# Scatter in one run and a runtime branch moved to the 13th expert block, in a two-layer mixer and MoE trunk

## The chip, the cores and the metric

The kernel runs on one core of a Trainium2 chip. The metric is device time in microseconds (us) of one execution. The kernel before takes 858.16 us, the median of three runs (857.32 to 858.34). One more execution was profiled; it took 858.35 us, and its trace covers a span of 856.6 us.

## The reference

The trunk has two layers for 256 tokens of width 1024, all in float32. A layer has a token mixer (one input projection; a causal convolution branch and a pooling branch, merged by gates; an output projection) and then a routed mixture of experts:

```
h2 = modulate(rms_norm(x, ffn_norm_g[l]), sh2, sc2)
x  = x + g2[:, None, :] * hierarchical_moe(h2, ...)

# hierarchical_moe: top-1 of 4 groups, top-2 of the 8 experts in it
combine = sum(one_hot(expert_id, 32) * weights[..., None], axis=1)
act = silu(t @ w_g[e]) * (t @ w_u[e])            # 1024 -> 256 per expert
out = out + (act * combine[:, e]) @ w_d[e]       # 256 -> 1024
```

So each token uses two of 32 experts. Each expert has 3 MB of weights, which every execution reads from HBM: about 101 MB per layer.

## The kernel before

**Layer.** `mixer` does the first half of a layer. `route` then finds each token's experts, gives every (token, expert) pair a place in a packed list of 512 columns sorted by expert, and gathers the normalised tokens into those columns (`XTp`, two tiles, tags `wl0` and `wl1`). `experts` and the function `blocks` that it returns do the rest.

**Blocks.** The 32 experts are worked in 16 blocks of two (`b` = 0 to 15). An expert has a window of 64 packed columns (`CAP`). `window(b)` (L1044, ScalarE) copies both windows into `XTW[b % 2]`. A block then does, on TensorE: gate/up (L1106, 32 matmuls, two 64-column halves of the array side by side), two transposes of the activated result (L1121), and down (L1081, 16 matmuls in two halves of 512 output columns). ScalarE and VectorE work between them: `sl` is silu (L1115) times up times routing weight (L1116), `aT` is the copy of the transposes (L1123), `gain` (L1087, L1088) multiplies down's result by the layer's gain and rounds it to a high part `yh`, `rest` (L1092) makes the low part `yl`.

**Scatter.** A block's 128 result rows go back to their tokens by a matrix of zeros and ones (`GT`, made by `prep`, L1052 and L1053). There are four parts, two halves of the columns for each of two token tiles; `scatter(b, part)` does two matmuls each (L1061 with `yh`, L1062 with `yl`), and `add(b, part)` (L1069, VectorE) adds the result to the residual `xs`. The scatter of block b - 1 is done in block b: parts 0 and 1 between gate/up and the transposes, parts 2 and 3 between the transposes and down. Parts and down share the PSUM pool `pd` of three buffers, except in the last block, whose parts 2 and 3 take `pa`.

**Overflow.** If an expert has over 64 tokens, its window doesn't hold them. `windows` (L821) computes a flag for that, and `overflow` (L977) loads it into a register of TensorE, ScalarE, VectorE and GpSimd (L980) and branches over a long body (L981) that would work all 32 experts for the tokens left out. On these inputs the body isn't run: the trace has none of its instructions. `overflow` is called at the end of `experts` (L1180), ahead of `blocks`. The body's weight loads go through GpSimd's queue; its working memory is `XTW[1]` and a tile of tag `xn`, the tag that `yhl` has in the blocks.

**Order.** In `route` and in the body of `experts` the order on TensorE, VectorE, ScalarE and GpSimd is the written one (`manual_schedule`). In blocks 0 to 14 only TensorE's is; VectorE and ScalarE are ordered by the compiler's scheduler. The end of block 15 is written for all four. An `If` is one unit of the schedule.

**Loads.** SP issues all weight loads in one fixed order, into a ring of 14 buffers of 1 MB, with up to five spare places for most of the experts. A load is issued when `done` frees a buffer, and waits for the release. A block uses six: gate and up of both experts in two halves of the input rows (512 KB loads, L114), and two for down (L116). After layer 0's experts the loads of the next layer follow at once.

Of the kernel before, what the change touches and what calls it, by code (L numbers as in the profile page):

```python
# [42 lines left out]
         1: ((0, 0), (0, 1), 0, 1, 4, 2, 5, 3, 6, 7, (1, 0), (1, 1))}  # L43
DIV_DVE = {0, 1, 2, 3}
FILL = (12, 24)
TAPS1, TAPS2 = 7, 6
ON_DVE = {2, 4, 6, 8, 30, 32, 34, 35, 36, 38}

# [2 lines left out]
def trunk(ctx, tc, x, c, mixer_norm_g, w_ada, b_ada, w_in, conv_w, conv_b, conv_ln_g, conv_ln_b,  # L51
# [643 lines left out]
    def route(l, moe, out_mm, out_add):  # L695
# [8 lines left out]
        def rt(name, shape, dt=F32):  # L704
            n = 1
            for d in shape[1:]:
                n *= d
            w = n // 2 if dt == BF else n
            v = rtile[:, rtop[0]:rtop[0] + w]
            rtop[0] += w  # L710
            if dt != F32:
                v = v.bitcast(dt)
            return v.rearrange(*{2: ("p a -> p a",), 3: ("p (a b) -> p a b",), 4: ("p (a b c) -> p a b c",)}[len(shape)],
                               **dict(zip("abc"[:len(shape) - 2], shape[1:-1])))
# [13 lines left out]
        ov = rt("ov", [P, TT, NE])  # L728
        px = rt("px", [P, TT, NE])
        po = rt("po", [P, TT, 2, NE])  # L730
        pk = rt("pk", [P, TT, 2])
        code = rt("code", [P, 2, TT, 2])
        so = rt("so", [P, NE])
        si = rt("si", [P, NE], I32)
# [76 lines left out]
            nc.vector.tensor_reduce(out=dst, in_=po, axis=AX.X, op=OP.add)  # L811

        def place():
            pick(pk, r["rp"][:, :TT, :])
            for ch in range(NCHUNK):
                if ch:
                    nc.vector.tensor_scalar(pk, pk, float(-SPC), None, op0=OP.add)
                for tt in range(TT):
                    onehot(G2[:, ch], tt, pk[:, tt, :])

        def windows():  # L821
            nc.vector.tensor_scalar(so, r["rp"][:, 2, :], float(LAST), None, op0=OP.min)
# [35 lines left out]
                        nc.vector.tensor_scalar(dst, p[:, kk, :], s["A2"][:, k:k + 1], s["B2"][:, k:k + 1],  # L858
                                                op0=OP.mult, op1=OP.add)

        r = dict(XTp=XTp, rss=rss, lg=lg, lm=lm, gm=gm, em=em, O=O, ov=ov, po=po, code=code, si=si, rt=rt, fill=fill)
        out_mm(2, 0)
        out_mm(3, 0)
        out_add(0)
# [112 lines left out]
    def overflow(l, r, moe):  # L977
        s = L[l]
        eng = [E.PE, E.Activation, E.DVE, E.Pool]
        flag = nc.values_load(r["fl"][0:1, 0:1], engines=eng, min_val=0, max_val=1)  # L980
        with tc.If(flag > 0):  # L981
            xo = work.tile([P, 2, D], F32, name="xo", tag="xn")
            xn = xo[:, 0].rearrange("p (k m) -> p k m", k=KC)
            hT = xo[:, 1].rearrange("p (k t) -> p k t", k=KC)
            wsp = r["XTW"][1].rearrange("p a c -> p (a c)")
            wov = r["lm"]
            nc.vector.tensor_tensor(wov, r["cw"][:, :, 0], r["cw"][:, :, 1], op=OP.add)
            nc.vector.tensor_tensor(wov, r["ov"], wov, op=OP.mult)
            for tt in range(TT):
                nc.scalar.activation(xn, xs[:, tt, :].rearrange("p (m k) -> p k m", k=KC), AF.Identity,  # L990
                                     scale=r["rss"][tt])
                for h in range(2):
                    p = pa([P, 4, P])
                    for kk in range(4):
                        nc.tensor.transpose(p[:, kk, :], xn[:, 4 * h + kk, :], ident)
                    for kk in range(4):
                        k = 4 * h + kk
                        nc.vector.tensor_scalar(hT[:, k, :], p[:, kk, :], s["A2"][:, k:k + 1], s["B2"][:, k:k + 1],
                                                op0=OP.mult, op1=OP.add)
                for e in range(NE):  # L1000
                    p = pa([P, 2, DE])
                    for i, wsrc in enumerate((w_expert_gate, w_expert_up)):
                        wv = wsrc[l, e].rearrange("(p k) h -> p k h", k=KC)
                        for h in range(2):
                            w = wsp.rearrange("p (k h) -> p k h", h=DE)
                            nc.gpsimd.dma_start(out=w, in_=wv[:, 4 * h:4 * h + 4, :])
                            for kk in range(4):
                                k = 4 * h + kk
                                nc.tensor.matmul(p[:, i, :], hT[:, k, :], w[:, kk, :], start=k == 0, stop=k == KC - 1)
                    sl = moe.tile([P, DE], F32, name="sl")  # L1010
                    nc.scalar.activation(sl, p[:, 0, :], AF.Silu)
                    ac = sl
                    nc.vector.scalar_tensor_tensor(ac, sl, wov[:, tt, e:e + 1], p[:, 1, :], op0=OP.mult, op1=OP.mult)
                    q = pt([P, 2, P])
                    for h in range(2):
                        nc.tensor.transpose(q[:, h, :], ac[:, h * P:(h + 1) * P], ident)
                    aT = moe.tile([P, 2, P], F32, name="aT")
                    nc.vector.tensor_copy(aT, q)
                    o = [pd([P, 512]) for _ in range(2)]
                    for h in range(2):  # L1020
                        nc.gpsimd.dma_start(out=wsp, in_=w_expert_down[l, e].rearrange("(j p) n -> p j n", p=P)[:, h])
                        for n in range(2):
                            nc.tensor.matmul(o[n], aT[:, h, :], wsp[:, n * 512:(n + 1) * 512], start=h == 0, stop=h == 1)
                    for n in range(2):
                        ns = slice(n * 512, (n + 1) * 512)
                        t = two.tile([P, 512], F32, name="ot", tag="part", bufs=3)
                        nc.vector.tensor_tensor(t, o[n], s["g2"][:, ns], op=OP.mult)
                        nc.vector.tensor_tensor(xs[:, tt, ns], xs[:, tt, ns], t, op=OP.add)


    def experts(l, r, moe):
# [23 lines left out]
        def scatter(b, part):  # L1055
            if b < 0:
                return
            h, tt = divmod(part, 2)
            hs = slice(h * 512, (h + 1) * 512)
            o = outs[part] = (pa if b == nb - 2 and part > 1 else pd)([P, 512])  # L1060
            nc.tensor.matmul(o, GTs[b][:, tt, :], ys[b][0][:, hs], start=True, stop=False)  # L1061
            nc.tensor.matmul(o, GTs[b][:, tt, :], ys[b][1][:, hs], start=False, stop=True)  # L1062

# [32 lines left out]
        def blocks():  # L1096
          with tc.manual_schedule(engines={E.PE}):
            for b in range(nb):
                p = pb([P, 2, DE])
                XT = XTW[b % 2]  # L1100
                for h in range(2):
                    w = need(*(("gu", l, 2 * b + j, h) for j in range(2)))
                    for kk in range(4):
                        k = 4 * h + kk
                        for j in range(2):
                            nc.tensor.matmul(p[64 * j:64 * j + 64], XT[:, k, 64 * j:64 * j + 64],  # L1106
                                             w[j][:, :, kk, :], start=k == 0, stop=k == KC - 1)
                    for j in range(2):
                        done(("gu", l, 2 * b + j, h))
                if b == 0:  # L1110
                    spread(r)
                    prep(0)
                window(b + 1)
                sl = moe.tile([P, DE], F32, name="sl", bufs=1)
                nc.scalar.activation(sl, p[:, 0, :], AF.Silu)  # L1115
                nc.vector.scalar_tensor_tensor(sl, sl, r["ws"][:, b:b + 1], p[:, 1, :], op0=OP.mult, op1=OP.mult)  # L1116
                scatter(b - 1, 0)
                scatter(b - 1, 1)
                q = pt([P, 2, P])
                for h in range(2):  # L1120
                    nc.tensor.transpose(q[:, h, :], sl[:, h * P:(h + 1) * P], ident)  # L1121
                aTs[b] = moe.tile([P, 2, P], F32, name="aT", bufs=1)
                nc.vector.tensor_copy(aTs[b], q)  # L1123
                add(b - 1, 0)
                add(b - 1, 1)
                scatter(b - 1, 2)
                scatter(b - 1, 3)
                add(b - 1, 2)
                add(b - 1, 3)
                prep(b + 1)  # L1130
                yhl = work.tile([P, 2, D], F32R, name="yhl", tag="xn")
                ys[b] = (yhl[:, 0, :], yhl[:, 1, :])
                if b == nb - 1:
                    break
                for n in range(2):
                    down(b, n)
                    gain(b, n)
                    rest(b, n)
                for j in range(2):
                    done(("ed", l, 2 * b + j))  # L1140
                if b == 5 and l + 1 < DEPTH:
                    small_mix(l + 1)
                if l + 1 == DEPTH and b in (5, 9):
                    final_gain(b)
# [32 lines left out]
        weights(l, r)  # L1177
        r["fill"](100)
        flush()
        overflow(l, r, moe)  # L1180
        return blocks


# [76 lines left out]
```

## Time and profile before

| | |
|---|---|
| time, median of 3 | 858.16 us |
| profiled execution | 858.35 us, span 856.6 us |
| TensorE busy | 775.5 us, 91% of the span |
| VectorE busy | 503.3 us, 59% |
| ScalarE busy | 279.7 us, 33% |
| GpSimd busy | 214.2 us, 25% |
| HBM read | 296.29 MB, 347 GB/s over the span |
| gate/up, L1106 | 912 matmuls, 228.1 us |
| down, L1081 | 512 matmuls, 160.6 us |
| adds, L1069 | 124, 82.1 us |
| GpSimd's load queue | 128 packets, 0.02 MB |

Matmuls are pipelined and overlap, so a matmul's own time (601 ns in gate/up) is longer than the step from one to the next. Layer 0's blocks run from about 210 to 436 us of the span, layer 1's from 618 to 845.

### The profile page before, as it was taken

The numbers are of one execution on the slowest core, as the hardware profiler recorded it, in microseconds if no ns is written. First come the engines' busy times: TensorE is split into PE (matmuls) and PEld (weight loads), VectorE is DVE, ScalarE is ACT, GpSimd is POOL, SyncE is SP. The second block draws the span as 40 slices with busy tenths as digits, with TensorE's granted clock in tenths as the row PEclk, the third lists the DMA queues.
The fourth block names the chain that finished last, engine by engine and source line by source line (L and its number), as shares of the span: only waits on it lengthen the run. The fifth ranks groups of instructions, "written<-read, shape, count | busy, mean of one in ns | idle before, by whom it ended". The sixth has DMA issues, their size and how long they took to land. (4 is left out here: it accounts for less than half of the span.)

```text
span 856.6 us, 12068 instructions
## 1 busy us (share of the span) xinstructions
PE 775.5 (91%) x4382; PEld 444.5 (52%) x4382; DVE 503.3 (59%) x1007; ACT 279.7 (33%) x496; POOL 214.2 (25%) x151
## 2 busy tenths in 40 slices
PE   4599999989799999999979999999679999999995
PEld 1389986755233333333339998686533333333332
DVE  2359984976245545454566998497734454535454
ACT  2254544454222122212135444545422212222212
POOL 1168972540000000000034799162100000000001
PEclk9699999999899999999988999999889999999998
DMA  9999958979999999999999965797679999999981
GB/s 350 371 355 390 390 172 335 353 250 404 404 406 409 408 409 366 354 409 410 404 380 382 397 226 186 283 385 248 241 249 372 383 410 409 409 409 409 409 347 49
DMA packets 100083, 298.28 MB, mean 348 GB/s; under 512 B 13941, under 2 KB 23461, under 8 KB 100010
## 3 DMA queue, kind: packets, MB, share of 16 engines
q1 hardware_dynamic: 99448, 296.30, 90.9%
q10 hardware_dynamic: 434, 1.06, 0.3%
q8 instruction: 38, 0.62, 0.3%
q14 instruction: 35, 0.29, 0.1%
q0 software_dynamic: 128, 0.02, 0.0%
HBM read 296.29 MB, written 1.05 MB: 347 GB/s over the span
## 5 line engine op out<-in xcount | busy, mean ns | idle before, releaser
L1106 PE MATMUL pb<-wt,XTW 128*64 128x512 f32 x912 | 228.1, 601 | 10.1 <-PEq L981 9.1
L427 POOL TENSOR_TENSOR wlo<-wt,whi 128x1024 fp32r<-128x1024 f32 x60 | 147.0, 2463 | 90.4 <-ACT whi L425 66.6
L1069 DVE TENSOR_TENSOR xs<-xs,pd 128x512 f32<-128x512 f32 x124 | 82.1, 684 | 134.8 <-PE pd L1062 133.6
L1106 PEld LDWEIGHTS pb<-wt,XTW 128*64 128x64 f32 x912 | 72.9, 139 | 132.2 <-issue 126.5
L486 DVE SCALAR_TENSOR_TENSOR pd<-vpad,cols,pd 128x256 f32<-128x256 f32 x232 | 106.9, 488 | 5.7
L425 ACT CAST whi<-wt 128x1024 fp32r<-128x1024 f32 x80 | 83.0, 1050 | 73.8 <-PE pb L365 40.8
L1088 ACT CAST yhl<-y 128x512 fp32r<-128x512 f32 x64 | 39.6, 620 | 195.1 <-DVE y L1087 195.1
L1081 PE MATMUL pd<-wt,aT 128*64 128x512 f32 x320 | 94.9, 598 | 0.9 <-DVE aT L1123 0.5
L1044 ACT COPY XTW<-XTp 128x256 f32 x128 | 48.3, 406 | 131.8 <-PE pb L1106 120.3
L1092 DVE TENSOR_TENSOR yhl<-y,yhl 128x512 fp32r<-128x512 f32 x64 | 44.3, 693 | 46.1 <-ACT yhl L1088 46.0
L364 PE MATMUL pa<-hhl,whi 128*128 128x256 f32 x224 | 66.5, 297 | 5.2 <-ACT hhl L399 5.2
L316 PE MATMUL pd<-wt,cb 128*32 128x512 f32 x384 | 54.3, 655 | 14.6 <-DMA wt<-in_w_ada_dram 14.5
L1081 PE MATMUL pd<-wx,aT 128*64 128x512 f32 x192 | 65.7, 598 | 0.5 <-DVE aT L1123 0.5
L365 PE MATMUL pa<-hhl,whi 128*128 128x256 f32 x224 | 65.8, 294 | 0.3
L366 PE MATMUL pa<-hhl,wlo 128*128 128x256 f32 x224 | 64.7, 289 | 0.7 <-POOL wlo L427 0.7
L364 PE MATMUL pb<-hhl,whi 128*128 128x256 f32 x224 | 63.6, 284 | 0.0
L365 PE MATMUL pb<-hhl,whi 128*128 128x256 f32 x224 | 62.7, 280 | 0.0
L366 PE MATMUL pb<-hhl,wlo 128*128 128x256 f32 x224 | 62.6, 279 | 0.0
L1061 PE MATMUL pd<-yhl,GT 128*128 128x512 f32 x124 | 54.9, 443 | 0.6 <-ACT yhl L1088 0.6
L1081 PEld LDWEIGHTS pd<-wt,aT 128*64 128x64 f32 x320 | 27.0, 136 | 52.8 <-issue 37.2
L1168 POOL TENSOR_TENSOR xn<-xs,fz 128x512 f32<-128x512 f32 x2 | 2.6, 1284 | 189.9 <-ACT xn L353 189.9
L1087 DVE TENSOR_TENSOR y<-pd,gb 128x512 f32<-128x512 f32 x64 | 44.0, 688 | 9.9 <-PE pd L1081 9.7
(260 smaller groups left out, 1249.7 us busy)
## 6 DMA issues: line engine op xcount, KB each, us to landing
wt<-in_w_expert_gate_dram SPq DMA_DIRECT2D x114, 512.0 KB, 7.1
wt<-in_w_expert_up_dram SPq DMA_DIRECT2D x114, 512.0 KB, 11.7
wt<-in_w_ada_dram SPq DMA_DIRECT2D x48, 1024.0 KB, 11.7
wt<-in_w_expert_down_dram SPq DMA_DIRECT2D x36, 1024.0 KB, 12.4
wt<-in_w_in_dram SPq DMA_DIRECT2D x28, 1024.0 KB, 13.9
wx<-in_w_expert_down_dram SPq DMA_DIRECT2D x24, 1024.0 KB, 12.7
wt<-in_w_out_dram SPq DMA_DIRECT2D x8, 1024.0 KB, 4.9
wx<-in_w_expert_gate_dram SPq DMA_DIRECT2D x14, 512.0 KB
```

Of the source, the lines that this page charges most:

```text
L316: nc.tensor.matmul(ps[j:j + 32, :], cb[:, 2 * i + a, :], halves(w[:, a, :], h), start=i == 0, stop=i == 3)
L364: nc.tensor.matmul(o, ah, bh, start=start, stop=False, skip_group_check=True)
L365: nc.tensor.matmul(o, ah, bl, start=False, stop=False, skip_group_check=True)
L366: nc.tensor.matmul(o, al, bh, start=False, stop=stop, skip_group_check=True)
L425: nc.scalar.copy(hi, wv)
L427: eng.tensor_tensor(lo, wv, hi.bitcast(F32), op=OP.subtract)
L486: nc.vector.scalar_tensor_tensor(acc[:, j, :] if t == CONV_K - 1 else a, src, w, a, op0=OP.mult, op1=OP.add)
L1044: nc.scalar.copy(XTW[b % 2][:, 4 * h:4 * h + 4, CAP * j:CAP * j + CAP], r["XTp"][h][:, :, bass.ds(v, CAP)])
L1061: nc.tensor.matmul(o, GTs[b][:, tt, :], ys[b][0][:, hs], start=True, stop=False)
L1069: nc.vector.tensor_tensor(xs[:, tt, hs], xs[:, tt, hs], outs.pop(part), op=OP.add)
L1081: nc.tensor.matmul(o[64 * j:64 * j + 64, :], aTs[b][:, h, 64 * j:64 * j + 64], wv[j][:, h, :], start=h == 0, stop=h == 1)
L1106: nc.tensor.matmul(p[64 * j:64 * j + 64], XT[:, k, 64 * j:64 * j + 64], w[j][:, :, kk, :], start=k == 0, stop=k == KC - 1)
```

## The change

Three edits. First, all four scatter parts of block b - 1 come between gate/up and the transposes of block b, and the four adds behind `aT`; parts 0 and 1 use the PSUM pool `pa` (two buffers), parts 2 and 3 `pd`. Second, `overflow` is called in `blocks`, ahead of block 12 (`LATE`), and the scatter of block 11 is done in front of it, so that block 12 has none. Third, the body of the branch works on the four sets of 128 packed columns in `XTp` instead of normalising the tokens anew; for that, `place` keeps both chunks' places in `pk`. The flag that decides on the body is computed as before.

```
+LATE = 12
...
-        pk = rt("pk", [P, TT, 2])
+        pk = rt("pk", [P, NCHUNK, TT, 2])
...
-            pick(pk, r["rp"][:, :TT, :])
+            pick(pk[:, 0], r["rp"][:, :TT, :])
             for ch in range(NCHUNK):
                 if ch:
-                    nc.vector.tensor_scalar(pk, pk, float(-SPC), None, op0=OP.add)
+                    nc.vector.tensor_scalar(pk[:, 1], pk[:, 0], float(-SPC), None, op0=OP.add)
                 for tt in range(TT):
-                    onehot(G2[:, ch], tt, pk[:, tt, :])
+                    onehot(G2[:, ch], tt, pk[:, ch, tt, :])
...
-            o = outs[part] = (pa if b == nb - 2 and part > 1 else pd)([P, 512])
+            o = outs[part] = (pa if part < 2 else pd)([P, 512])
...
             for b in range(nb):
+                if b == LATE:
+                    for part in range(4):
+                        scatter(b - 1, part)
+                        add(b - 1, part)
+                    overflow(l, r, moe)
                 p = pb([P, 2, DE])
...
-                scatter(b - 1, 0)
-                scatter(b - 1, 1)
+                if b != LATE:
+                    for part in range(4):
+                        scatter(b - 1, part)
                 q = pt([P, 2, P])
                 for h in range(2):
                     nc.tensor.transpose(q[:, h, :], sl[:, h * P:(h + 1) * P], ident)
                 aTs[b] = moe.tile([P, 2, P], F32, name="aT", bufs=1)
                 nc.vector.tensor_copy(aTs[b], q)
-                add(b - 1, 0)
-                add(b - 1, 1)
-                scatter(b - 1, 2)
-                scatter(b - 1, 3)
-                add(b - 1, 2)
-                add(b - 1, 3)
+                if b != LATE:
+                    for part in range(4):
+                        add(b - 1, part)
                 prep(b + 1)
...
         r["fill"](100)
         flush()
-        overflow(l, r, moe)
         return blocks
```

## Rows read from the trace of the kernel before

**Rows 1.** Chain of waits from 625 us on: shares by line, and one later piece.
```profile
by line: PE pb L1106 12.9%; PE pd L1081 6.5%; PE pd L1061 1.4%; DVE xs L1069 1.3%; PE pd L1062 1.1%; PE pt L1121 0.7%; DVE sl L1116 0.7%; PE pd L1195 0.2%; ACT xn L353 0.2%; DVE yhl L1092 0.2%; issue 0.2%; DVE y L1087 0.2%; PE pd L966 0.1%;
...
652.85 6.87 PE pb L1106 x32
```

**Rows 2.** Timeline, layer 1's block 1: start, us, instruction, count, [idle before, releaser].
```profile
645.99 0.50 PE L1061 MATMUL pd<-yhl,GT 128*128 128x512 f32 x1
...
646.56 0.40 PE L1061 MATMUL pd<-yhl,GT 128*128 128x512 f32 x1
...
646.76 0.69 DVE L1069 TENSOR_TENSOR xs<-xs,pd 128x512 f32<-128x512 f32 x1 [4.45 <-PE pd L1062]
646.80 0.39 PE L1062 MATMUL pd<-yhl,GT 128*128 128x512 f32 x1
...
647.36 0.47 DVE L1116 SCALAR_TENSOR_TENSOR sl<-sl,rtile,pb 128x256 f32<-128x256 f32 x1
647.75 0.68 DVE L1069 TENSOR_TENSOR xs<-xs,pd 128x512 f32<-128x512 f32 x1
...
647.89 0.44 PE L1121 MATMUL pt<-idc,sl 128*128 128x128 f32 x2 [0.71 <-DVE sl L1116]
...
648.37 0.42 DVE L1123 COPY aT<-pt 128x256 f32<-128x256 f32 x1
...
649.19 3.65 PE L1081 MATMUL pd<-wx,aT 128*64 128x512 f32 x16
```

**Rows 3.** Timeline, the last two blocks of layer 1.
```profile
825.55 0.50 PE L1061 MATMUL pd<-yhl,GT 128*128 128x512 f32 x1
...
828.17 3.65 PE L1081 MATMUL pd<-wt,aT 128*64 128x512 f32 x16 [0.17 <-DVE xs L1069]
...
838.62 0.50 PE L1061 MATMUL pd<-yhl,GT 128*128 128x512 f32 x1
...
838.74 0.39 ACT L1115 ACTIVATE sl<-pb 128x256 f32<-128x256 f32 x1 [5.20 <-PE pb L1106]
...
840.17 0.42 DVE L1123 COPY aT<-pt 128x256 f32<-128x256 f32 x1
...
841.00 3.65 PE L1081 MATMUL pd<-wt,aT 128*64 128x512 f32 x16
```

**Rows 4.** Timeline, TensorE around the branch of layer 1.
```profile
617.98 2.79 PE L1106 MATMUL pb<-wt,XTW 128*64 128x512 f32 x10 [1.02 <-ACT XTW L1044]
...
625.06 7.60 PE L1106 MATMUL pb<-wt,XTW 128*64 128x512 f32 x22 [4.30 <-PEq L981]
```

**Rows 5.** Line 981 by sequencer (q): count, ns minimum/median/maximum, first and last start.
```profile
L981 POOLq EVENT_SEMAPHORE  x8: 17/43/43, 203.4 to 612.1; - x8
L981 POOLq COMPARE_BRANCH  x2: 45/48/50, 197.9 to 609.3; - x2
...
L981 PEldq COMPARE_BRANCH  x2: 6102/6118/6133, 212.6 to 618.8; - x2
```

**Rows 6.** Line 980 on TensorE's sequencer.
```profile
L980 PEldq TENSOR_LOAD <-rtile x2: 310/400/490, 211.7 to 613.4; - x2
```

**Rows 7.** Stretches: busy us (count) by engine, then PEclk, DMA share, GB/s.
```profile
626.00:628.00 2.00, 2.00 (x8) 0.74 (x6) 0.60 (x4) 0.83 (x3) 0.00 (x0) 0.50 0.00 0
```

**Rows 8.** Page, part 2: GB/s in 40 slices of 21.4 us.
```profile
GB/s 350 371 355 390 390 172 335 353 250 404 404 406 409 408 409 366 354 409 410 404 380 382 397 226 186 283 385 248 241 249 372 383 410 409 409 409 409 409 347 49
```

**Rows 9.** Timeline, TensorE in layer 0: block 11's gate/up, and the end of block 15.
```profile
369.40 7.04 PE L1106 MATMUL pb<-wt,XTW 128*64 128x512 f32 x32
...
432.82 3.65 PE L1081 MATMUL pd<-wt,aT 128*64 128x512 f32 x16
...
438.97 0.51 PE L1062 MATMUL pd<-yhl,GT 128*128 128x512 f32 x1 [0.23 <-DVE yhl L1092]
```

**Rows 10.** Timeline of SP, layer 0: one load's issue.
```profile
354.56 0.33 SPq L114 DMA_DIRECT2D wt<-in_w_expert_up_dram  x1
```

**Rows 11.** Loads issued from 417 to 422 us: count, size each, median us to landing.
```profile
wt<-in_w_expert_down_dram SPq DMA_DIRECT2D x4, 512.0 KB, 10.4
```

More of the change, by code (lines that the diff above doesn't have):

```diff
@@ L859, in gather @@
                                                 op0=OP.mult, op1=OP.add)
-        r = dict(XTp=XTp, rss=rss, lg=lg, lm=lm, gm=gm, em=em, O=O, ov=ov, po=po, code=code, si=si, rt=rt, fill=fill)
+        r = dict(XTp=XTp, rss=rss, lg=lg, lm=lm, gm=gm, em=em, O=O, ov=ov, pk=pk, po=po, code=code, si=si, rt=rt, fill=fill)
         out_mm(2, 0)
@@ L982, in overflow @@
             xo = work.tile([P, 2, D], F32, name="xo", tag="xn")
[L983 to L999, printed above, removed]
+            wsp, y = xo[:, 0], xo[:, 1]
@@ new lines, in overflow @@
+            nc.vector.tensor_tensor(r["cw"], r["cw"], r["ov"][:, :, None, :].to_broadcast([P, TT, 2, NE]), op=OP.mult)
+            for c in range(2 * SEQ // P):
+                at = slice(c % 2 * P, c % 2 * P + P)
+                g = two.tile([P, TT, 2, P], F32, name="gp", tag="part", bufs=3)
+                for tt in range(TT):
+                    for i in range(2):
+                        nc.vector.tensor_scalar(g[:, tt, i, :], io256[:, at], r["pk"][:, c // 2, tt, i:i + 1], None,
+                                                op0=OP.is_equal)
+                pw = pt([P, NE])
+                for n in range(4):
+                    nc.tensor.matmul(pw, g[:, n // 2, n % 2, :], r["cw"][:, n // 2, n % 2, :], start=n == 0, stop=n == 3)
+                wv = two.tile([P, NE], F32, name="wv", tag="b2s", bufs=1)
+                nc.vector.tensor_copy(wv, pw)
+                gt = two.tile([P, TT, P], F32, name="gt", tag="part", bufs=3)
+                for tt in range(TT):
+                    nc.vector.tensor_tensor(g[:, tt, 0, :], g[:, tt, 0, :], g[:, tt, 1, :], op=OP.add)
+                    q = pt([P, P])
+                    nc.tensor.transpose(q, g[:, tt, 0, :], ident)
+                    nc.vector.tensor_copy(gt[:, tt, :], q)
+                o = [pd([P, 512]) for _ in range(2)]
@@ L1002, in overflow @@
                     for i, wsrc in enumerate((w_expert_gate, w_expert_up)):
-                        wv = wsrc[l, e].rearrange("(p k) h -> p k h", k=KC)
+                        wx = wsrc[l, e].rearrange("(p k) h -> p k h", k=KC)
                         for h in range(2):
                             w = wsp.rearrange("p (k h) -> p k h", h=DE)
-                            nc.gpsimd.dma_start(out=w, in_=wv[:, 4 * h:4 * h + 4, :])
+                            nc.gpsimd.dma_start(out=w, in_=wx[:, 4 * h:4 * h + 4, :])
                             for kk in range(4):
-                                k = 4 * h + kk
-                                nc.tensor.matmul(p[:, i, :], hT[:, k, :], w[:, kk, :], start=k == 0, stop=k == KC - 1)
+                                nc.tensor.matmul(p[:, i, :], r["XTp"][h][:, kk, c * P:(c + 1) * P], w[:, kk, :],
+                                                 start=h + kk == 0, stop=h + kk == 4)
                     sl = moe.tile([P, DE], F32, name="sl")
@@ L1012, in overflow @@
                     ac = sl
-                    nc.vector.scalar_tensor_tensor(ac, sl, wov[:, tt, e:e + 1], p[:, 1, :], op0=OP.mult, op1=OP.mult)
+                    nc.vector.scalar_tensor_tensor(ac, sl, wv[:, e:e + 1], p[:, 1, :], op0=OP.mult, op1=OP.mult)
                     q = pt([P, 2, P])
@@ L1018, in overflow @@
                     nc.vector.tensor_copy(aT, q)
-                    o = [pd([P, 512]) for _ in range(2)]
                     for h in range(2):
@@ L1022, in overflow @@
                         for n in range(2):
[L1023 to L1028, printed above, removed]
+                            nc.tensor.matmul(o[n], aT[:, h, :], wsp[:, n * 512:(n + 1) * 512],
+                                             start=e + h == 0, stop=e + h == NE)
+                for n in range(2):
+                    ns = slice(n * 512, (n + 1) * 512)
+                    nc.vector.tensor_tensor(y[:, ns], o[n], s["g2"][:, ns], op=OP.mult)
+                    for tt in range(TT):
+                        q = pa([P, 512])
+                        nc.tensor.matmul(q, gt[:, tt, :], y[:, ns], start=True, stop=True)
+                        nc.vector.tensor_tensor(xs[:, tt, ns], xs[:, tt, ns], q, op=OP.add)
     def experts(l, r, moe):
```

## The prediction, made before the result was known

> **What bounds the kernel now.** I read the chain of waits first: from the first expert block of the second layer to the end it runs along TensorE, through gate/up (L1106), down (L1081), scatter and transposes, with two VectorE instructions per block and no load in it [rows 1]. Then the timeline of one block [rows 2]. Gate/up ends at 645.99, the next down begins at 649.19. In these 3.20 us TensorE issues two scatter parts (four matmuls from 645.99 to 646.80, 0.24 apart once they run), waits 0.71 us for `sl`, transposes, issues two more parts and goes on. The wait is VectorE's: an add of 0.60 stands ahead of `sl` in its queue. Thirteen of a layer's sixteen blocks look like this; in the last two `sl` comes ahead of the add, and the gaps are 2.62 and 2.38 us [rows 3]. Third, the branch: after ten gate/up matmuls of block 0 TensorE of layer 1 stands 4.30 us behind its sequencer, whose branch takes 6.1 us in both layers [rows 4, 5]. It restarts at half clock: 22 matmuls take 7.60 us, against 22 x 0.215 = 4.73 at full clock (6.87 / 32 each) [rows 1, 4, 7]. Last the loads: layer 0's blocks, from 205 to 430 us, run on a saturated queue, 404 to 410 GB/s outside two slices, while in layer 1 the queue falls to 241 and 249 around the branch [rows 8].
>
> **The change part by part.** The sum is made against the profiled execution, 858.35 us (span 856.6 and 1.75 around it); the median shown is 0.19 below.
>
> *No branch at the start.* Without it the eleventh matmul would issue 0.22 after the tenth, which issues near 620.18 (its modelled end 620.77 less 0.59), not at 625.06: 4.7 us earlier. The clock loss, 7.60 - 4.73 = 2.9, goes too. I take 7.5 us, and the same for layer 0, where the branch is as long. What is late next is block 0's chain behind gate/up, which stays as it is. The eight mask instructions of `spread` on VectorE then run under gate/up.
>
> *Four scatter parts in one run.* From 645.99: four matmuls to 646.80, four more at 0.24 to 647.76, transposes at 648.00, `aT` 0.48 later as now (647.89 to 648.37), 0.42 of copy and 0.05, down at 648.95. The gap becomes 2.96: 0.24 saved in an ordinary block. `sl`, done at 647.75, hides under the scatter, but the cover that `aT` had, the two scatter parts behind the transposes, is gone: its 0.47 lies bare, and that is why so little is won. In the last two blocks 2.96 replaces 2.62 and 2.38, 0.34 and 0.58 lost. The parts that move to the other PSUM pool find it free, as nothing else in blocks 1 to 15 uses it. The second down half now takes the buffer of part 2 and waits for its add, which ends about 1.2 us after `aT` begins, under the 1.79 us of the first half. Blocks 1 to 11 give 11 x 0.24 = 2.6; blocks 13 to 15 together cost 0.34 + 0.58 - 0.24 = 0.7.
>
> *Block 12.* Let t be the end of down(11). The scatter of block 11 now runs with no gate/up over it. The last block of layer 0 shows that price: down begins at 432.82 and takes 3.6 (649.19 to the next gate/up), which ends it at 436.4, and the last scatter wait is met at 438.97, t + 2.57 [rows 2, 9]. Then the flag load and the branch: 0.9 from load to branch (211.7 to 212.6) and 6.1 [rows 5, 6], 0.2 to the first matmul: t + 9.8. The scatter's last matmuls end under it, so TensorE stands some 6 us and the clock falls: gate/up takes 6.87 + 2.8, to t + 19.5. No scatter follows, so the gap is the bare chain, 0.05 + 1.43 from `silu` to `aT` [rows 3] + 0.47: down(12) at t + 21.4. Before it began at t + 6.87 + 3.20 = t + 10.1, so the cost is 11.3. That is the upper end if TensorE keeps to the written order. But in the kernel before, ten gate/up matmuls that are written behind the branch ran ahead of it [rows 4]; five ahead would fill the time in which VectorE ends its adds, 1.1 us, for 10.2. Nothing tells between the two; I take 10.8. Below that lies only a cheaper branch, which is a rival. The other engines reach their branch at t + 2 (ScalarE) to t + 5 (VectorE) and need it past at t + 19. On POOL nothing of the blocks is queued behind it. SP has no branch; its loads behind block 12's releases come later, and the loads of more than two blocks are ahead of them (14 buffers, 6 per block).
>
> *The load queue.* In layer 1 it was not full at the start, because loads waited for block 0's buffers; an earlier start moves loads and matmuls together, and nothing is lost. In layer 0 it is saturated, so an earlier TensorE runs into it. Counted back from the layer's last, block 11's last gate/up load is issued at 354.56; at 10.4 us to landing it is there at 365.0, and TensorE wants it half way through gate/up, 369.40 + 3.43 = 372.8 [rows 9 to 11]. That is 7.9 us of lead, while the advance by then is 7.5 + 10 x 0.24 = 9.9. The two slices at 366 and 354 GB/s [rows 8] may partly fill up when buffers come free earlier, worth 0 to 2.5 us; I take 1. So 1.0 us of the advance is lost in layer 0.
>
> *The rest.* The copy of the places for the second chunk costs one small VectorE instruction, as before. The rewritten body runs nothing as long as the flag is zero, as now.
>
> Sum, layer 1: -7.5 - 2.6 + 0.7 + 10.8 = +1.4. Layer 0: the same and 1.0, +2.4; the next layer starts on the residual, so it passes on. Together +3.8, or 862.1 against 858.35, and **862.0** against the median. With the ends 10.2 and 11.3 for block 12 and 0 to 2.5 for the slices this case spans 860 to 864, and with 0.1 us of error in the gap (26 blocks) 857.5 to 866.5.
>
> [...]
>
> **Rivals.**
> *VectorE puts an add ahead of `aT`.* Its order in the blocks isn't written by hand. The second add ends at 648.37 [rows 2], `aT` would be ready at 648.48, and the third add, whose scatter is now early, is ready before both. If whoever is ready goes first, `aT` waits 0.5 more, and the gap is 3.46, 0.26 longer than now. For: the add that stands ahead of `sl` today. Against: the margin is 0.1 us, and in the last two blocks `aT` did come ahead of the second add. Price 14 x 0.5 = 7.0 per layer, less layer 0's 1.0, since nothing runs into the queue then: +3.8 + 14.0 - 1.0 = +16.8, 875.
>
> *The branch is cheaper at block 12: faster.* The skip isn't one price for all: POOL was past it in 2.8 us in layer 1 (609.3 to 612.1) and in 5.5 in layer 0 (197.9 to 203.4) [rows 5]. If TensorE's 6.1 were 2.8 there, 3.3 us go per layer, and up to 2.8 more if so short a stand leaves the clock up: 862 - 6.6 = 855.4 to 849.8, middle 853. It decides from 1.9 us per layer, a branch of 4.2. Against: TensorE took 6.1 with a saturated queue in layer 0 and with a queue running dry in layer 1, and block 12 has a saturated one.
>
> *The branch moves and costs the same.* Should the scheduler run gate/up(12) and the bare chain under the branch, block 12 costs about 8.5 to 9.5, and the kernel ends within 0.2% of before: 858.5.
>
> **How the numbers follow.** Forecast case 0.53, the add ahead of `aT` 0.25, the cheaper branch 0.13, the hidden one 0.09. A measurement of this kernel tells 0.2% (1.7 us) from no change. The forecast case, by its span, is slower in 0.36, the same in 0.13, faster in 0.04. The second case is slower; the third is faster but for 0.02; the fourth gives 0.06 same, 0.01 slower, 0.02 faster. Slower 0.62, same 0.21, faster 0.17. The range reaches from the upper end of the cheaper branch, 855, to just above the late `aT`, 876; the forecast's own is 857.5 to 866.5.
>
> **What would show it.** Right: no stand in block 0 and its gate/up at full clock; a gap of 2.96 with no wait for `sl`; in block 12 a stand of 5 to 6 us behind the sequencer and a clock of 0.5 after it; in layer 0 a short wait for gate/up weights near block 11. Wrong: an add between `sl` and `aT` twice over (second case); a branch far from 6.1 us; more than ten gate/up matmuls ahead of it; or a layer 0 that ends earlier than at 436 us, as its queue allows almost nothing.

## The result, and the profile after

The changed kernel takes 867.6 us (median of four runs, 865.2 to 869.8) against 858.16, the median of the three ordinary runs of before (a fourth took 1570.39 us and is left out): ratio 1.0108, 95% interval 1.009 to 1.0125. It is 9.4 us slower; 3.8 were forecast. A second measurement, beside the experiments, gave 1.0095 (1.0064 to 1.0127). The profiled execution is 867.54 us, 9.19 above that of before.

One row per step of the prediction, each from first matmul to first matmul (us, after minus before, from the two timelines; down(11) is the first down matmul of block 11):

```
                                    layer 0                   layer 1                  forecast
gather -> first down          22.77 - 29.98 =  -7.2    23.48 - 29.84 =  -6.4      -7.5
first down -> down(11)       147.31 - 150.19 = -2.9   148.67 - 152.25 = -3.6      -2.6 (+1.0 in layer 0)
down(11) -> down(12)          31.48 - 13.65 = +17.8    24.44 - 13.65 = +10.8     +10.8
down(12) -> down(15)          39.95 - 39.60 =  +0.4    39.96 - 39.55 =  +0.4      +0.7
sum                                           +8.1                     +1.2      +2.4, +1.4
```

One cell stands out, down(11) to down(12) in layer 0. Its ends, in the kernel before and in the changed one:

```profile
365.92 3.65 PE L1081 MATMUL pd<-wt,aT 128*64 128x512 f32 x16
379.57 0.64 PE L1081 MATMUL pd<-wt,aT 128*64 128x512 f32 x1
```
```profile
370.77 0.64 PE L1088 MATMUL pd<-wt,aT 128*64 128x512 f32 x1 [0.52 <-DVE aT L1136]
...
402.25 0.65 PE L1088 MATMUL pd<-wx,aT 128*64 128x512 f32 x2 [0.52 <-DVE aT L1136]
```

An ordinary block first, as in [rows 2] (timeline of layer 1's block 1 in the changed kernel: start, us, instruction, count, idle before and releaser):

```profile
647.27 0.50 PE L1068 MATMUL pa<-yhl,GT 128*128 128x512 f32 x1
...
648.65 0.47 DVE L1128 SCALAR_TENSOR_TENSOR sl<-sl,rtile,pb 128x256 f32<-128x256 f32 x1
...
649.02 0.39 PE L1069 MATMUL pd<-yhl,GT 128*128 128x512 f32 x1
649.04 0.68 DVE L1076 TENSOR_TENSOR xs<-xs,pa 128x512 f32<-128x512 f32 x1
...
649.24 0.38 PE L1134 MATMUL pt<-idc,sl 128*128 128x128 f32 x2
649.67 0.42 DVE L1136 COPY aT<-pt 128x256 f32<-128x256 f32 x1
650.01 1.27 DVE L1076 TENSOR_TENSOR xs<-xs,pd 128x512 f32<-128x512 f32 x2
...
650.14 1.08 PE L1088 MATMUL pd<-wx,aT 128*64 128x512 f32 x4 [0.52 <-DVE aT L1136]
```

Eight scatter matmuls in one run, no wait for `sl`, the third and fourth add behind `aT`, and 2.87 us from scatter to down where it was 3.20. Now the branch, by sequencer, as in [rows 5], and what TensorE does behind it in layer 0:

```profile
L982 PEldq COMPARE_BRANCH  x2: 5972/6036/6100, 378.3 to 792.8; - x2
```
```profile
384.74 1.09 PE L1118 MATMUL pb<-wx,XTW 128*64 128x512 f32 x1 [6.35 <-DMA wx<-in_w_expert_down_dram]
390.44 1.01 PE L1118 MATMUL pb<-wx,XTW 128*64 128x512 f32 x1 [4.62 <-issue]
390.57 1.09 PE L1118 MATMUL pb<-wt,XTW 128*64 128x512 f32 x1
```

TensorE stands 6.35 us at the branch (a load is named as releaser; at the same place in layer 1 it is the sequencer), issues one matmul and stands again for 4.62, waiting for nothing that the profile ties to it. In layer 1 the same code runs on:

```profile
799.13 1.08 PE L1118 MATMUL pb<-wx,XTW 128*64 128x512 f32 x1 [6.03 <-PEq L982]
799.26 1.09 PE L1118 MATMUL pb<-wt,XTW 128*64 128x512 f32 x1
800.01 1.06 PE L1118 MATMUL pb<-wx,XTW 128*64 128x512 f32 x1
```

The view of the DMA queues lists what moved in a stretch: packets, MB, share of 16 engines. Inside the second stand (384.7 to 390.4 us) there are rows of kind instruction, that is, of code, and the page's third part has q8 for the whole span:

```profile
q8 instruction: 1, 0.02, 1.4%
q14 instruction: 2, 0.02, 0.9%
```
```profile
q8 instruction: 39, 0.64, 0.3%
```

39 packets for 0.64 MB are pieces of 16 KB of code. In ordinary blocks a q8 packet comes every two blocks or so: from 226.2 to 362.3 us they are 26.5 to 28.3 us apart, with 234 to 254 matmuls and weight loads of TensorE from one to the next. Behind the branch of layer 0 they begin at 381.9 and 387.7, each 2.7 to 2.8 us ahead of a restart. That q8 brings TensorE's code is read from these times and counts; which engines q14 serves, with its smaller packets, isn't shown. And each restart finds the clock at half (busy us and count, then the granted clock, DMA share, GB/s):

```profile
384.70:385.90 1.20, 1.09 (x1) 0.50 1.01 403
390.40:394.00 3.60, 3.56 (x9) 0.50 1.02 408
394.00:402.20 8.20, 6.74 (x27) 0.88 1.03 409
```

### The profile page after: what moved, and what is told of

It reads as the page before. It is cut to its first block, busy times and chain, and to the rows that moved or that the text cites. A ratio compares the mean times of both kernels' runs of the same rounds, so it can differ in the third digit from the quotient of the medians.

```text
span 865.7 us, 12039 instructions
## 1 busy us (share of the span) xinstructions
PE 776.0 (90%) x4382; PEld 455.3 (53%) x4382; DVE 499.5 (58%) x1007; ACT 279.1 (32%) x496; POOL 214.2 (25%) x151
## 5 line engine op out<-in xcount | busy, mean ns | idle before, releaser
L1118 PEld LDWEIGHTS pb<-wt,XTW 128*64 128x64 f32 x912 | 76.2, 138 | 124.0 <-issue 119.0
L1076 DVE TENSOR_TENSOR xs<-xs,pa 128x512 f32<-128x512 f32 x64 | 43.3, 684 | 124.7 <-PE pa L1069 124.7
L1118 PE MATMUL pb<-wx,XTW 128*64 128x512 f32 x112 | 52.5, 638 | 17.0 <-DMA wx<-in_w_expert_down_dram 6.4
```

## The experiments

Theory A: the second stand is a second fetch of code. The branch lands four or five instructions before the end of a piece, and the next one is asked for only then. B: the second matmul waits for weights on the full queue. C: it belongs to the place, block 12 of layer 0. D: the branch's 6 us are the compare itself, not a fetch. The test for A is code that never runs. How far the landing point is from the end of its piece is an estimate: I counted it in the program, with the end put where the changed kernel stands. Where nothing else is said, a fence shows TensorE's timeline of the kernel named, in the columns above.

**Moving the landing point** (`shift16`, `shift248`, `move_stand`, `start_stand`). One edit, with other counts per layer:

```diff
         with tc.If(flag > 0):
+            pad = (4, 0)[l]    # shift248 (62, 0); move_stand (4, 23); start_stand (43, 0), branch at the start
+            if pad:
+                q = pt([P, P])
+                for n in range(pad):
+                    nc.tensor.matmul(q, ident, ident, start=n == 0, stop=n == pad - 1)
```

> The changed kernel with four more matrix products in the body of layer 0's branch, which the flag never lets run: 17 instructions of TensorE that shift where the code behind both branches lies and change nothing that runs. Theory A (the second stand of layer 0, 4.62 us behind the first matmul of block 12, is a second fetch of code: the branch lands four or five instructions before the end of a fetched 16 KB piece): the landing point is now past that end, the stand goes, block 12 of layer 0 costs about what it costs in layer 1, and the kernel takes 867.6 less 5.7 to 7.1: 861 us (860 to 862.5). Theory B (the second matmul waits for a load of weights on the full queue): the stand stays, 867 to 868. Theory C (the place at block 12 of layer 0, whatever the code): the same 867 to 868.

Measured: 863.2 us, ratio 1.0042 (1.0024 to 1.006), where the changed kernel has 1.0108 and 1.0095; that is 0.7 us above the upper end of the expectation, and the profiled execution, 861.1, is the fastest of its ten. No second stand; down(11) to down(12) takes 25.06 in layer 0.

```profile
382.85 1.08 PE L1123 MATMUL pb<-wx,XTW 128*64 128x512 f32 x1 [6.36 <-PEq L982]
382.97 1.09 PE L1123 MATMUL pb<-wt,XTW 128*64 128x512 f32 x1
383.73 1.06 PE L1123 MATMUL pb<-wx,XTW 128*64 128x512 f32 x1
```

The next piece still comes (one q8 packet between 382.8 and 390 us), but beside running matmuls. B and C fall: nothing that runs was changed.

> The changed kernel with 249 never-run instructions in layer 0's body, so that the landing point of layer 0 has some seven more instructions left in its 16 KB piece than in the changed kernel: eleven or twelve. Theory A, with sizes: the next piece comes as late as before, some 5.7 us behind the restart, so the second stand begins later by what the seven instructions run and is shorter by the same: 2.5 to 3.5 us instead of 4.62, and the step from down(11) to down(12) 28 to 30.5 us instead of 31.48 (25.0 without a second stand). If the landing point were only lucky and nothing were counted by pieces: 25 or 31.5.

Measured, in a single execution: 867.8 us; the second stand is 3.61, just above the forecast, the step 29.36.

```profile
385.81 1.06 PE L1123 MATMUL pb<-wt,XTW 128*64 128x512 f32 x1
390.48 1.01 PE L1123 MATMUL pb<-wx,XTW 128*64 128x512 f32 x1 [3.61 <-issue]
```

More matmuls run first, and the second restart comes 5.73 us after the first (384.75), as in the changed kernel (5.70): the next piece takes the same time (in the changed kernel its q8 packet begins 5.8 us behind the first one's), the stand is what is left of it.

> The changed kernel with never-run matrix products in both bodies: 17 instructions in layer 0's (as in the run before, where the second stand went) and 93 in layer 1's, chosen so that layer 1's landing point has three or four instructions left before the end of a 16 KB piece, as layer 0's has in the changed kernel. Theory A (the second stand is the fetch of the next piece): layer 0 has no second stand, layer 1 has one of 4 to 5 us behind its first matmul of block 12, where the changed kernel has none; the step from down(11) to down(12) is 25 us in layer 0 and 30 to 31.5 in layer 1; in all about the changed kernel's time, 863.2 plus 5 to 6.5: 868 to 870 us. Theory C (the place in layer 0): no second stand in layer 1, 863 us. Rival: each body adds instructions of its own to the code that the count from the program does not hold, so that the landing point of layer 1 is missed: also 863 us, and then this run says nothing against A.

Measured: 865.8 us, ratio 1.0081 (1.0058 to 1.0104), below the 868 to 870 expected; layer 0's step is 24.95, layer 1's 27.17.

```profile
795.05 1.08 PE L1123 MATMUL pb<-wx,XTW 128*64 128x512 f32 x1 [6.13 <-DMA wt<-in_w_expert_up_dram]
...
796.78 1.91 PE L1123 MATMUL pb<-wx,XTW 128*64 128x512 f32 x2
800.37 0.59 PE L1123 MATMUL pb<-wt,XTW 128*64 128x512 f32 x1 [1.68 <-issue]
```

The stand moved into layer 1, where the changed kernel has none: against C. But it is 1.68 us, not 4 to 5, and begins some 15 instructions after the landing: my count of the code missed by 11 or 12 there. Why isn't settled. The second restart is again 5.3 us behind the first.

> The kernel with the branch at the start and the scatter in one run, with 173 never-run instructions in layer 0's body, so that the landing point at the start of layer 0 has four instructions left in its piece. Theory A: a second stand at the start of layer 0, behind its first gate/up matmul after the branch, of 3 to 5 us; from the first gather matmul to the first down 34 to 36.5 us instead of 30.2. As the last two blocks of layer 0 waited 3.4 us for loads without it, only part reaches the end: 857.1 plus 1 to 3, 858 to 860 us. Theory C (block 12 of layer 0 makes the stand): no second stand, 857 us.

Measured: 859.8 us, ratio 1.0005 (0.9992 to 1.0018). The stand can be put at the layer's start too; first gather matmul to first down takes 35.1 us, where the same kernel without never-run instructions (`scatters_only`, below) takes 30.25:

```profile
218.54 1.94 PE L1122 MATMUL pb<-wt,XTW 128*64 128x512 f32 x2 [4.64 <-PEq L982]
224.15 1.97 PE L1122 MATMUL pb<-wt,XTW 128*64 128x512 f32 x4 [3.67 <-issue]
```

The time lies in the forecast, but not for its reason: in the profile all of the stand reaches the end of layer 0, which takes 238.62 us from gather to down(15) against 233.46. The last two steps, 14.53 and 15.77, are as long as there (14.64 and 15.37).

**Taking the branch apart** (`no_branch`, `tiny_body`).

```diff
                         add(b - 1, part)
-                    overflow(l, r, moe)
```

> The changed kernel without flag and branch, so the overflow's work is left out; the scatter of block 11 still stands ahead of block 12's gate/up. Theory A (both stands are fetches behind the branch): first stands 6.35 and 6.03, second stand 4.62 and the half clock behind it all go: 867.6 less 12.4 less 7 and some clock, 846 to 849 us. Theory B or C (the second stand belongs to loads or to the place): only the first stands go, 854 to 856 us. What block 12 still costs here over an ordinary block is the price of the order alone, forecast 3.5 to 4.5 us a layer.

Measured: 852.6 us, ratio 0.991 (0.9877 to 0.9942), between the two forecasts. Both stands are gone; down(11) to down(12) takes 16.87 in both layers, so the order alone costs 16.87 - 13.32 = 3.5. What was not forecast is layer 0's end: its last three steps take 15.3 us instead of 13.3, and TensorE waits there for loads (waits of TensorE from 390 to 434 us: total, times, longest):

```profile
PE pb L1117 <- DMA wt<-in_w_expert_up_dram: 2.9, 3, 1.0
```

For `tiny_body` one VectorE instruction of the body stays:

```diff
             nc.vector.tensor_tensor(r["cw"], r["cw"], r["ov"][:, :, None, :].to_broadcast([P, TT, 2, NE]), op=OP.mult)
-            for c in range(2 * SEQ // P):
...
```

> The changed kernel with the branch kept on all four engines, but a body of a single VectorE instruction: the overflow's work is left out, and TensorE's branch jumps over nothing. Theory A (the 6.0 us of the branch are the fetch of code that lies 11,000 instructions further on): the branch falls to under 1 us a layer, no second stand, 847 to 850 us, within 2 us of the kernel without a branch. Rival D (the price is the register load, the compare and the redirect themselves, or the full queue that delays the flag): 5 to 6 us a layer stay, 859 to 861 us.

Measured: 851.9 us, ratio 0.9907 (0.9873 to 0.9941), 0.7 from the kernel without a branch; both lie above theory A's forecasts, as layer 0's last three steps are long here too (13.88, 15.51 and 15.40). D falls: on TensorE's sequencer the same branch over nothing takes (ns, minimum/median/maximum)

```profile
L982 PEldq COMPARE_BRANCH  x2: 207/216/224, 377.4 to 784.9; - x2
```

0.2 us instead of 6.0. Down(11) to down(12) is 17.32 and 17.03. So of the 25 us that this step takes without a second stand, some 7.8 are the fetch and the half clock after it (25.06 - 17.32, 24.84 - 17.03 in `shift16`), 3.5 the bare scatter, 13.3 the block, and the rest, 0.2 to 0.5 (17.03 and 17.32 less 16.87), the flag's load and the compare.

**One part alone** (`scatters_only`, `branch_only`).

```diff
         flush()
+        overflow(l, r, moe)
         return blocks
```

with the call at block 12 and its scatter taken out; for `branch_only` instead the old order of scatter and add.

> The four scatter parts in one run in every block, the branch back at the layer's start with the new body. Theory A: the gap is 0.3 to 0.35 us shorter in 11 to 14 blocks of each layer and the last two blocks give back 0.5 to 0.7 us, with the old price of the start: 858.3 less 6 to 8, 850 to 852 us. Rival E (the shorter gap of the changed kernel came with the missing start, not with the order): 857 to 859 us. Rival F (the longer body or its landing point costs a second stand at the start): 6 us a layer more, 856 to 864.

Measured: 857.1 us, ratio 0.9972 (0.9955 to 0.9988): about a third of the forecast gain. The time is rival E's, but its reason is not: each block is 0.33 shorter here too. Rival F falls as well: the start takes 30.25 and 30.00 us, before 29.98 and 29.84. In layer 1 the gain is there: from gather to down(15) 231.95 us, before 235.30. In layer 0 it is not: 233.46 and 233.42. From block 14 on the loads take it back:

```profile
422.18 4.46 PE L1117 MATMUL pb<-wt,XTW 128*64 128x512 f32 x18
427.65 3.62 PE L1117 MATMUL pb<-wt,XTW 128*64 128x512 f32 x14 [1.01 <-DMA wt<-in_w_expert_up_dram]
```

> The branch moved to block 12 with its new body, the scatter parts in the old order (two before the transposes, two behind). By the count its landing point in layer 0 has 249 instructions left. Theory A: no second stand; the start gives back 7.2 and 6.4 us, block 12 costs 11 to 11.5 us over an ordinary block in each layer: +8 to +9.5 us, 867 to 869 us. Theory C (a second stand belongs to block 12 of layer 0): 6.4 us more, 873 to 876 us.

Measured: 868.5 us, ratio 1.0112 (1.0094 to 1.013), as theory A says; no second stand in block 12 of layer 0, steps of 25.63 and 24.96.

**Versions that might beat both** (`mid`, `mid_mended`, `tail_old`). The branch behind block 12's scatter and transposes:

```diff
-                if b == LATE:
-                    for part in range(4):
-                        scatter(b - 1, part)
-                        add(b - 1, part)
-                    overflow(l, r, moe)
...
                 for part in range(4):
                     add(b - 1, part)
+                if b == LATE:
+                    overflow(l, r, moe)
```

> All four scatter parts in one run in every block; the branch still in block 12, but behind that block's scatter and transposes, so that gate/up covers the wait for yhl and only the fetch stays; the body keeps its activation and its transposed copy in free columns of its own buffer; 49 never-run instructions in layer 1's body keep the landing point away from the end of a piece. By the changed kernel's parts: start -6.4, gaps -3.9, branch +6.2 to +8, last blocks +0.4 in layer 1: -2 to -4; layer 0 as much, but its loads bound it, so -0.5 or so there: 854 to 857.5 us, 1 to 4 us under the kernel before. Rival G (VectorE's own branch, of 5.5 us, comes in front of what the next down needs): 3 to 6 us a layer worse, 860 to 866 us.

Measured: 862.9 us, ratio 1.0045 (1.0031 to 1.0059): missed, and by my own padding. In layer 1 the down after the branch waits not 6 us but 12:

```profile
802.15 1.12 PE L1093 MATMUL pd<-wt,aT 128*64 128x512 f32 x2 [12.15 <-DMA wt<-in_w_expert_gate_dram]
```

With the 11 or 12 instructions by which the count had missed in `move_stand`, the landing point would lie on the very end of a piece, so that two pieces are fetched in this one wait. That is an estimate; the next run tests it.

> The branch behind scatter and transposes of block 12, as in the run before, but with 81 instead of 49 never-run instructions in layer 1's body: with 49 the landing point of layer 1 fell on the end of a piece (its restart came 5.7 us late; the runs put that end 11 or 12 instructions further on in layer 1 than the count said). Theory A: layer 1's two steps behind down(11), 24.96 and 16.06 us, become layer 0's 21.5 and 14.7 or less: 862.9 less 4 to 6, 857 to 859 us. Rival G (the long wait in layer 1 was VectorE's branch or a load): 862 to 864 us as before.

Measured: 857.2 us, ratio 0.9971 (0.9953 to 0.999); the wait is 6.62, and rival G falls with it. The layer-1 steps are 19.43 and 15.59: the fetch costs 35.0 - 26.6 = 8.4 us in the middle of a block too, as the downs and the next gate/up start at a lower clock (in layer 0 of this run 0.50 from 390.7 to 394.0 us and 0.71 to 397.5).

```profile
797.62 1.12 PE L1093 MATMUL pd<-wt,aT 128*64 128x512 f32 x2 [6.62 <-DVE GT L1065]
```

The last: branch at the start, one run of scatter up to block 13, two parts and two parts in blocks 14 and 15.

```diff
-                for part in range(4):
+                for part in range(4 if b < nb - 2 else 2):
                     scatter(b - 1, part)
```

> The branch at the start, the scatter in one run up to block 13, and the old order in the last two blocks. Layer 1: the two last steps 13.1 and 12.8 to 12.9 us instead of 13.32 and 13.32, so 0.6 to 0.8 us less; layer 0 nothing, as its loads bound its end. 857.1 less 0.6 to 0.8: 856 to 857 us, ratio to the kernel before 0.995 to 0.998. Rival: the change of order between block 13 and 14 costs a wait on a PSUM tile, 0.5 to 1 us a layer: 857 to 859 us.

Measured: 854.7 us, ratio 0.9939 (0.9916 to 0.9961): faster than before and than the change. The last two steps of layer 1 are 13.06 and 12.82, as forecast; that is 0.7 us less than in `scatters_only`. How much of the lead over `scatters_only` this order gives is not shown: the two medians, from different measurements, lie 2.4 us apart, but from gather to down(15) the two profiles take the same (233.24 and 232.13 against 233.46 and 231.95), as layer 1's start is 0.9 longer here, and the 2.3 us between the two spans lie ahead of layer 0's gather and between the layers, where the two kernels have the same order.

```profile
811.08 0.64 PE L1088 MATMUL pd<-wt,aT 128*64 128x512 f32 x1 [0.52 <-DVE aT L1134]
...
824.14 3.65 PE L1088 MATMUL pd<-wt,aT 128*64 128x512 f32 x16 [0.17 <-DVE xs L1076]
...
836.96 1.51 PE L1088 MATMUL pd<-wt,aT 128*64 128x512 f32 x6
```

The run beside these, the changed kernel again:

> The changed kernel once more, beside the others of this call. If the run without the second stand (863.2, ratio 1.0042 to the kernel before) is to be set against it, the same ratio as at first is expected, 1.009 to 1.0125, and the same step of 31 to 32 us from down(11) to down(12) in layer 0 with an idle of 4.5 to 4.8 us behind the first matmul.

Measured: 868.8 us, ratio 1.0095; step 31.23, second stand 4.63.

## Why the prediction was wrong, step by step

The direction was right, the size not; one step carries the miss. "Block 12" was costed at 10.8 us for both layers, with one stand at the branch. Layer 1 measured 10.8. Layer 0 measured 17.8: there the branch lands at the end of a fetched piece and TensorE stands a second time, for 4.62 us, and then runs at half clock once more. The step took the restart as final, and "The rewritten body runs nothing as long as the flag is zero" took the body as free, while its length decides where the code behind it lies. Without the second stand, by `shift16`, the kernel is 3.9 us slower than before (1.0042), and the forecast was 3.8. That it comes so near is in part luck: from gather to down(15) `shift16` is 1.6 us slower in layer 0 and 2.2 in layer 1, where 2.4 and 1.4 were forecast. So is layer 1's 10.8: in `after_again`, `shift16` and `shift248` the same step is 24.84 to 24.97, so 11.2 to 11.3, the upper end.

The other terms. The start gave 7.2 and 6.4, not 7.5. The gap shrank by 0.33, not 0.24: from the first scatter matmul to the transposes it takes 1.97 us, not 2.01, and from there to `aT` 0.43, not 0.48. The third add came behind `aT`, so the second case is refuted. The last blocks cost 0.4, not 0.7. Layer 0's short wait for loads near block 11 was forecast at 1.0; there the step is 14.07, 0.75 over its neighbours. The cheaper branch is refuted: 5.97 to 6.10 us. Gate/up(12) did not run ahead of the branch, so the hidden branch is refuted as well, and the written order, the upper end of 11.3, held. Layer 1 came to 10.8 all the same, because the clock came back sooner than [rows 4] let expect: half for 2.6 us, full after 3.2, a loss of some 1.5 us where 2.8 was taken. Against that, ScalarE's copy of the next window (807.72 us) came ahead of the `silu` (808.03), which the bare chain didn't hold.

```profile
799.10:801.70 2.60, 2.57 (x6) 0.50 1.03 408
801.70:802.30 0.60, 0.60 (x4) 0.62 1.09 416
802.30:808.00 5.70, 5.45 (x26) 1.00 1.02 403
```

In ordinary blocks the next piece costs nothing that shows: q8 packets begin there too, and the steps stay at 13.32 us. Behind a branch that holds only if enough of the piece is left: with four, eleven and some fifteen instructions by my count the stand in block 12 was 4.62, 3.61 and 1.68 us, with a hundred and more none.

That layer 0's queue "allows almost nothing" held: only 1.1 us of all that `no_branch` saves there reaches the last down (232.36 against 233.42 from gather to down(15)). In the changed kernel this didn't show, because the branch had spent the advance before; it was the expectation for `scatters_only` that left it out.

## What to carry to other kernels

Price a skipped branch body by its code, not by what it runs: here 6 us of fetch on TensorE, some 2 of half clock, and up to 6.4 more (31.48 - 25.06) if the landing point lies near the end of a piece of code. Look for a second stand right behind a branch, and for a packet on the engine's queue of kind instruction, here q8, in the DMA view of that stretch; a few never-run instructions move the landing point, but a count from the program can miss: mine did by 11 or 12, and by the same estimate `mid` fell on the very end of a piece by its own padding. And before a saving on TensorE is counted, look whether the layer's loads leave room for it: on a queue at 400 to 406 GB/s (`no_branch`, 223 to 433 us) they took it back within three blocks.

## What the runs showed of the hardware that was not expected

A branch over a body of one VectorE instruction costs TensorE 0.21 us, over some 11,000 instructions of its own (counted in the program) 6.0 to 6.1; 6.1 before, over a body about half as long. Where TensorE stood a second time, the second restart came 5.3 to 5.7 us after the first (`after`, `shift248`, `move_stand`, and `start_stand` at the start of a layer). The time from the first q8 packet to the second isn't the same everywhere: in block 12 of the changed kernel it is 5.8 and 5.9 us (381.92 to 387.73, 796.35 to 802.25), at the start of layer 0 in the kernel before 5.9 (216.3 to 222.1), but at the start of layer 1 only 3.0 (622.5 to 625.5, where the load queue is down to 39 GB/s from 622 to 626). That the loads on the queue make the difference is not shown.
